# One transfer for the vectors and the first half of x, one for the first weights, decay preparation on GpSimd, and a bank read and three weight transfers placed sooner

## The chip, the core and the metric

The kernel runs on one core of one Trainium2 chip. A core has five engines with an instruction queue each: TensorE (PE in the profile; its weight loads are PEld), VectorE (DVE), ScalarE (ACT), GpSimd (POOL), and SyncE (SP), which here only asks for DMA transfers. The data lies in SBUF, 128 partitions wide; matmuls write to banks of PSUM. The metric is the device time of one execution in microseconds, as the median of several.

## What is computed

One layer of a hybrid decoder on 1024 tokens of width 1024, all in float32:

```python
z = rms_norm(h, norm_mix_g)
proj = z @ w_in                                  # 1024 -> 1536
y_pool = multiscale_pool_mixer(u_pool, ...)      # windows 2, 4, 8, 16
xb = causal_depthwise_conv(u_lru, conv_w, conv_b)
y_lru = rg_lru(xb, ...) * gelu(u_gate)           # log_a = 8 * r * log_sigmoid(lru_L)
h = h + concat([y_pool, y_lru]) @ w_out
z = rms_norm(h, norm_mlp_g)
h = h + square(relu(z @ w_up)) @ w_down          # 1024 -> 4096 -> 1024
z = rms_norm(h, norm_ple_g)
h = h + sigmoid(z @ w_ple_gate + b) * (p @ w_ple_proj)
return rms_norm(h, norm_final_g)
```

## The kernel before, in words

Activations stand transposed: the 1024 channels of x are eight tiles `H[k]` of 128 partitions, 1024 tokens wide. Every float32 product is made of three passes of a rounded format: an operand is split into a part `hi` (ScalarE, `split`, lines 180 and 183) and a rest `lo` (VectorE, lines 181 and 184), and `mm` (line 352) issues hi*hi, hi*lo and lo*hi as 128x512 matmuls. So nearly all matmuls have the same shape, and each needs a split by ScalarE and one by VectorE ahead of it. Weights come as raw tiles, two at a time, and their splits too lie in two buffers.

**The opening.** `vecs`, 80 columns of gains and biases (`COLS` names them), comes on ScalarE's queue (line 367). Nine matmuls on a tile `heat` keep TensorE busy meanwhile. Then a loop over k (line 487) loads `H[k]` and the weights `wl{k}` of the first projection (the recurrent channels): `H[0]` and `H[1]` in two halves of 512 tokens, the weights `wl0` in two cuts of 384 and 128 columns. All of these go through SyncE's queue, in the order of the program. For k = 0 the twelve matmuls of the first half come first, then the nine of the second half.

**Decay preparation.** `softplus` (line 454) works on tiles of 128x4: from `lru_L` it makes -8 log_sigmoid as `cpos` and its negative `cneg`, through an exponential on ScalarE and a series of nine steps, two operations each. It is issued at k = 2 on VectorE. `cneg` and `cpos` are first read by ScalarE in `lru_scan` (lines 612 and 613); `pool_bs`, the bias times the scale of the pooling mixer, in `pool_mix` (line 665).

**The mixer.** `project(i)` makes 48 matmuls into banks of PSUM. `normed` (line 552) reads the banks out on VectorE, times the inverse norm. `lru_gates(o)` makes twelve matmuls of 64 rows (line 592) into banks from the same pool, so these wait until an earlier result has been read out. The line in question is `normed(T[0], ps)` (line 689) after `lru_gates(2)`: it reads the result of `project(4)`, whose banks `lru_gates(3)` takes.

**The MLP.** Both products use a scheme with seven in place of eight block products (P1 to P7). The up product runs over 16 pairs of row tiles; `finish_up` (line 785) turns each pair's sums into operands of the down product and returns `store_up`, which writes them to DRAM tiles `act` by four transfers. The down product runs over the kinds P1, P2, P4, P6, P7, P5, P3, each with four steps q of 24 matmuls (`down`, line 960), twice. Its weights W[ij, q] are raw tiles loaded by `load_w`, its operands `wd` tiles X loaded back from `act` by `load_x` (line 295) and split by `prepare`. At P4 VectorE makes the sums that the later kinds take, first `w21 = w11 - w21` (line 214): that needs W[2, q]. W[2, 0] and W[2, 1] lie in T[2] and T[3], the tiles from which the last pair's first two stores read.

**What sets the order.** Within an engine the instructions run in the order that a scheduler has set from the program, with `tc.high_priority`, `tc.issue_after` and `pin` as means to move single ones. SyncE's queue is one such order: a transfer that has to wait for something holds up all transfers behind it.

Of the kernel before, what the change touches and what calls it, by code (L numbers as in the profile page):

```python
# [7 lines left out]
F32 = mybir.dt.float32  # L8
# [3 lines left out]
ALU = mybir.AluOpType  # L12

P = 128
S = 1024
D = 1024
DFF = 4096
HALF = 512
# [3 lines left out]
URGENT = 200  # L22
# [7 lines left out]
NT = D // P  # L30
# [9 lines left out]
NPOOL = 4  # L40
# [15 lines left out]
NVEC = _n  # L56
# [3 lines left out]
def block_kernel(  # L60
# [1 line left out]
    tc: tile.TileContext,  # L62
    xT: bass.AP,
    pT: bass.AP,
    vec: bass.AP,
    rows: bass.AP,
    w_lru: bass.AP,
    w_in: bass.AP,
# [9 lines left out]
    nc = tc.nc  # L78
# [5 lines left out]
    def fixed(name, dt):  # L84
        return pool.tile([P, S], dt, name=name)

    h_all = pool.tile([P, NT, S], F32, name="h")
    H = [h_all[:, i] for i in range(NT)]
    t_all = pool.tile([P, 6, S], F32, name="t")
    T = [t_all[:, i] for i in range(6)]  # L90

# [9 lines left out]
    def space(name, n, dt, side="left"):  # L101

        spaces[name] = ExitStack()
        sb = spaces[name].enter_context(tc.tile_pool(name=name, bufs=1, side=side))
        return [sb.tile([P, S], dt, name=f"{name}{i}") for i in range(n)]
# [5 lines left out]
        return list(zip(tiles[::2], tiles[1::2]))  # L111

    R = fixed("rstd", F32)
    dram = ctx.enter_context(tc.tile_pool(name="act", bufs=1, space=bass.MemoryType.DRAM))

    ACT = [
# [49 lines left out]
    def col(name, i):  # L166
        c = COLS[name] + i
        return vecs[:, c : c + 1]
# [3 lines left out]
    def pin(ins):  # L172
        return tc.keep_in_program_order(ins) if in_order else ins
# [3 lines left out]
    def split(src, hi, lo, g=None, eng=None):  # L177

        if g is None:
            first = pin(nc.scalar.activation(hi, src, AF.Copy))  # L180
            lowest[:] = [pin((eng or nc.vector).tensor_tensor(lo, src, f32(hi), ALU.subtract)).ins]  # L181
        else:
            first = pin(nc.scalar.activation(hi, src, AF.Identity, scale=g))
            lowest[:] = [pin(nc.vector.scalar_tensor_tensor(lo, src, g, f32(hi), ALU.mult, ALU.subtract)).ins]
        return first.ins

    def raw_tile(name):
        return wp.tile([P, S], F32, tag="raw", name=f"{name}_raw")
# [98 lines left out]
    def load_w(c, ij, q):  # L287
        if c < NCHUNK:
            nc.sync.dma_start(W[ij, q], w_down[c, ij, q])
# [73 lines left out]
        return t[:, k * P : (k + 1) * P]  # L363


    vecs = pool.tile([P, NVEC], F32, name="vecs")
    nc.scalar.dma_start(vecs, vec)
    heat = pool.tile([P, P], BF16, name="heat")
    tc.keep_in_program_order(nc.vector.memset(heat, 1.0))
    nc.vector.memset(T[4][:, :P], 1.0)  # L370
# [82 lines left out]
    def softplus():  # L453

        c0 = COLS["lru_l"]
        lv = vecs[:, c0 : c0 + NLRU]
        with tc.issue_after(lowest[0]):
            nc.vector.tensor_scalar_mul(neg, lv, -1.0)
        nc.vector.tensor_tensor(e, lv, neg, ALU.max)
        nc.scalar.activation(e, e, AF.Exp, scale=-1.0)  # L460
        nc.vector.tensor_scalar_add(s, e, 2.0)
        nc.vector.reciprocal(s, s)
        nc.vector.tensor_tensor(s, s, e, ALU.mult)
        nc.vector.tensor_tensor(s2, s, s, ALU.mult)
        nc.vector.memset(poly, 1.0 / 19)
        for n in range(8, -1, -1):
            nc.vector.tensor_tensor(poly, poly, s2, ALU.mult)
            nc.vector.tensor_scalar_add(poly, poly, 1.0 / (2 * n + 1))
        nc.vector.tensor_tensor(poly, poly, s, ALU.mult)
        nc.vector.tensor_scalar(neg, neg, 0.0, 8.0, ALU.max, ALU.mult)  # L470
        nc.vector.scalar_tensor_tensor(cpos, poly, 16.0, neg, ALU.mult, ALU.add)
        nc.vector.tensor_scalar_mul(cneg, cpos, -1.0)

        c_b, c_s = COLS["pool_b"], COLS["pool_s"]
        with tc.issue_after(lowest[0]):
            nc.vector.tensor_tensor(pool_bs, vecs[:, c_b : c_b + NPOOL], vecs[:, c_s : c_s + NPOOL], ALU.mult)

    norm = Norm("n0", T[0], T[1:3])
    ps_n = bank("n0_ps")
# [5 lines left out]
    for k in range(NT):  # L485
        halves = HALVES if k < 2 else (slice(0, S),)
        if k == 1:
            whi, wlo = weights()
        for hs in halves:
            begin = k == hs.start == 0  # L490
            nc.sync.dma_start(H[k][:, hs], xT[k * P : (k + 1) * P, hs])
            if begin:
                raw = raw_tile("wl0")[:, :HALF]
                whi, wlo = (t[:, :HALF] for t in weight_tiles("wl0"))
                cuts = slice(0, 3 * P), slice(3 * P, HALF)
                for cut in cuts:
                    nc.sync.dma_start(raw[:, cut], w_lru[:P, cut])
                pin(nc.vector.tensor_copy(whi[:, cuts[0]], raw[:, cuts[0]]))
            split(H[k][:, hs], A[k][0][:, hs], A[k][1][:, hs], col("g_mix", k))
            if k > 1:  # L500
                whi, wlo = weights()
            if begin:
                cut = cuts[0]
                pin(nc.vector.tensor_tensor(wlo[:, cut], raw[:, cut], f32(whi[:, cut]), ALU.subtract))
                split(*(t[:, cuts[1]] for t in (raw, whi, wlo)))
        for i in AFTER[k] if k < len(AFTER) else (k,):
            norm.add(H[i])
        if k == NT - 1:
            in_order.clear()
            ask()  # L510
        if k == 2:
            softplus()
        if k == 3:
            tables()
        if k == 5:
            pin(nc.scalar.activation(spread[:, 71:72], eps, AF.Sqrt))
        if k < 2:

            for hs in HALVES:
                for o in range(3):  # L520
                    mm(ps_l[o], kblk(whi, o), kblk(wlo, o), *A[k], k == 0, False, hs)
                if hs == FIRST:
                    mm([(FIRST, ps_four)], kblk(whi, 3), kblk(wlo, 3), *A[k], k == 0, False)
            continue
        for o in range(3):
            if k == NT - 1 and o == 2:
                norm.rstd(R, norm.sums((FIRST,), into=ps_n))
            mm(ps_l[o], kblk(whi, o), kblk(wlo, o), *A[k], False, k == NT - 1)
# [21 lines left out]
    def normed(dst, parts):  # L550
        for hs, ps in parts:
            nc.vector.tensor_tensor(by(dst[:, hs], ps), got(ps), by(R[:, hs], ps), ALU.mult)

# [132 lines left out]
    pool_windows(2, None)  # L686
    ps = project(4)
    lru_gates(2)
    normed(T[0], ps)
    ps = project(5)  # L690
    last = lru_gates(3)
    with tc.issue_after(last):
# [261 lines left out]
    def down(n):  # L954
        c, kind = KINDS[n]
        last = c == NCHUNK - 1

        def operand(t):
            return half(A[4 * (n % 2) + t // 2], t % 2)

        for q in range(NQ):
            w = weights() if n or q else asked.pop(0)
            if last and kind == "P5":
                if q == 0:
                    for k in range(2):
                        nc.sync.dma_start(T[4 + k], pT[k * P : (k + 1) * P, :])
                        nc.sync.dma_start(T[2 + k], w_proj[k * P : (k + 1) * P, :])
                elif q == 2:
                    open_ple()
            c11, c12, c21, c22 = (H[d][:, hs] for d in (2 * q, 2 * q + 1) for hs in HALVES)  # L970
            u = T[q // 2][:, HALVES[q % 2]]
            x = mlp_bank(f"ps_{kind}_d{c}_{q}")
            product(x, w, operand, range(CHUNK // 2), CHUNK // 2)
            if n == q == 0:
                leave("w0")
                S2[:] = *space("s2", 2, F32), *T[4:]
                finish_up(*done.pop())()
                for ij, i in ((1, 2), (1, 3), (3, 0), (2, 0), (3, 1), (2, 1)):
                    load_w(0, ij, i)
            if n == 1 and q in (1, 2):  # L980
                for ij in (3, 2):
                    load_w(0, ij, 1 + q)
            if kind == "P1":
                copy(u, x)
                add_got(c11, x)
            elif kind == "P2":
                add_got(c11, x)
            elif kind == "P6":
                add_got(u, x)
                add(c12, u)  # L990
            elif kind == "P7":
                add_got(u, x)
                add(H[2 * q + 1].rearrange("p (y s) -> p y s", y=2), twice(u))
            elif kind == "P4":
                add_got(c21, x)
            elif kind == "P5":
                add_both(h_all[:, 2 * q : 2 * q + 2, SECOND], x)
            else:
                add_got(c12, x)
            for tp in AHEAD[q] if n else AHEAD[q - 1]:  # L1000
                prepare(n + 1, tp)
            if last:
                for o in IN.get((kind, q), ()):
                    ple_in(o, FIRST, norm2)
                if (kind, q) == ("P3", 2):
                    norm2.casts((FIRST,))
# [392 lines left out]
```

## Time and profile before

| what | us |
|---|---|
| median of 3 runs | 922.6 (922.36 to 922.85) |
| the profiled execution, its own time | 922.75 |
| its span in the profile | 921.0 |
| TensorE busy in the span | 911.3 |
| VectorE busy | 762.5 |
| ScalarE busy | 444.5 |
| GpSimd busy | 8.0 |

The span runs from the first instruction to the last; 1.75 us of the profiled execution's time lie around it. A row of a timeline gives the start in us from the span's start, the time taken, the engine, the line, what it writes and reads, and in brackets how long the engine sat idle before it and what ended that. The letter q behind an engine is its queue: SPq rows are transfers being asked for, not their landing.

### The profile page before, as it was taken

Reading aid. Unit: us, or ns where it says so; the run is one execution under the profiler, and the core shown is the slowest. Engines: PE = TensorE matmul, PEld = TensorE weight load, DVE = VectorE, ACT = ScalarE, POOL = GpSimd, SP = SyncE. Lnnn points to the kernel's source line nnn. Section 1 sums busy time; section 2 is a strip of 40 time slices with the busy share of each in tenths; the row PEclk is TensorE's granted clock in tenths of the full one; section 3 lists DMA queues with packets and bytes.
Section 4 is the critical chain, followed back from the end, with each engine's and each line's share of the span. In section 5 each row is a group of like instructions: output and inputs, shape, how many; then the busy total and the mean of one; then the engine's idle time right before and its main releaser. Section 6 shows DMA issues by size and latency. Waiting matters only on the chain.

```text
span 921.0 us, 10988 instructions
## 1 busy us (share of the span) xinstructions
PE 911.3 (99%) x4229; PEld 792.4 (86%) x4229; DVE 762.5 (83%) x914; ACT 444.5 (48%) x516; POOL 8.0 (1%) x11
## 2 busy tenths in 40 slices
PE   9999999999999999999999999999999999999996
PEld 7888888888888888888888888888888888888886
DVE  7998984659998888888888989979777579789666
ACT  6567992447543343334333654444343346556223
POOL 0000000002000000000000000000000000000001
PEclk9999999999999999999999999999999999999999
DMA  7210143111245345435533988356533341031353
GB/s 272 93 54 32 38 161 114 69 46 51 88 166 189 126 154 195 154 126 175 198 131 145 315 329 328 129 186 203 192 123 119 114 161 46 1 121 63 105 174 121
DMA packets 50180, 129.07 MB, mean 140 GB/s; under 512 B 4560, under 2 KB 10192, under 8 KB 50128
## 3 DMA queue, kind: packets, MB, share of 16 engines
q1 hardware_dynamic: 49984, 128.34, 40.5%
q8 instruction: 33, 0.54, 0.2%
q14 instruction: 19, 0.16, 0.1%
q10 hardware_dynamic: 144, 0.04, 0.0%
HBM read 92.71 MB, written 35.65 MB: 139 GB/s over the span
## 4 chain that ended last, share of the span: by engine, by line
PE 85%; DVE 8%; DMA 3%; ACT 2%; issue 2%; SPq 0%; POOLq 0%; POOL 0%; ACTq 0%; DVEq 0%
PE ps_P_u L352 30%; PE ps_P_d L352 28%; PE ps_o L352 9%; PE ps_e L352 8%; PE ps_i L352 3%; PE ps_l L352 3%; PE ps_e L1163 2%; DMA wd<-act 2%; DVE h L565 2%; PE ps_j L352 1%; DMA wd<-in_w_down 1%; DVE y L181 1%; DVE wi_lo L181 1%; DMA h<-in_xT 1%; DVE t L647 1%
## 5 line engine op out<-in xcount | busy, mean ns | idle before, releaser
L352 PE MATMUL ps_P_d<-a,wd_P_hi 128*128 128x512 f32 x880 | 261.7, 379 | 0.0
L352 PEld LDWEIGHTS ps_P_d<-a,wd_P_hi 128*128 128x128 f32 x880 | 166.3, 189 | 23.6
L352 PE MATMUL ps_P_d<-a,wd_P_lo 128*128 128x512 f32 x440 | 166.9, 379 | 1.0 <-DVE wd_P_lo L181 1.0
L352 PE MATMUL ps_P_u<-a,wu_hi 128*128 128x512 f32 x512 | 152.3, 379 | 0.0
L352 PE MATMUL ps_P_u<-y,wu_hi 128*128 128x512 f32 x384 | 114.2, 379 | 0.0
L352 PEld LDWEIGHTS ps_P_u<-a,wu_hi 128*128 128x128 f32 x512 | 96.8, 189 | 13.8
L352 PE MATMUL ps_P_u<-a,wu_lo 128*128 128x512 f32 x256 | 97.0, 379 | 0.0
L352 PEld LDWEIGHTS ps_P_d<-a,wd_P_lo 128*128 128x128 f32 x440 | 83.2, 189 | 13.1 <-DVE wd_P_lo L181 1.4
L352 PEld LDWEIGHTS ps_P_u<-y,wu_hi 128*128 128x128 f32 x384 | 72.6, 189 | 10.3
L771 DVE TENSOR_TENSOR t<-t,ps_P_u 128x512 f32<-128x512 f32 (+1 forms) x80 | 62.5, 782 | 20.4 <-PE ps_P_u L352 20.4
L352 PE MATMUL ps_P_u<-y,wu_lo 128*128 128x512 f32 x192 | 72.8, 379 | 0.0
L180 ACT ACTIVATE a<-wd 128x1024 fp32r<-128x1024 f32 x56 | 59.0, 1055 | 24.2 <-DMA wd<-act 15.8
L181 DVE TENSOR_TENSOR a<-wd,a 128x1024 fp32r<-128x1024 f32 x56 | 67.2, 1220 | 1.0 <-ACT a L180 0.6
L352 PE MATMUL ps_i<-a,wi_hi 128*128 128x512 f32 x256 | 66.1, 381 | 0.0
L352 PE MATMUL ps_o<-y,wo_hi 128*128 128x512 f32 x256 | 65.7, 379 | 0.0
L180 ACT ACTIVATE wu_hi<-wu 128x1024 fp32r<-128x1024 f32 x24 | 25.4, 1058 | 69.8 <-PE ps_P_u L352 44.1
L180 ACT ACTIVATE wu_hi<-wu_raw 128x1024 fp32r<-128x1024 f32 (+1 forms) x26 | 25.3, 975 | 66.3 <-PE ps_P_u L352 41.3
L352 PEld LDWEIGHTS ps_i<-a,wi_hi 128*128 128x128 f32 x256 | 48.1, 189 | 8.0 <-issue 0.7
L352 PEld LDWEIGHTS ps_P_u<-a,wu_lo 128*128 128x128 f32 x256 | 48.4, 189 | 6.9
L352 PEld LDWEIGHTS ps_o<-y,wo_hi 128*128 128x128 f32 x256 | 48.4, 189 | 6.8
L180 ACT ACTIVATE wd_P_hi<-wd 128x1024 fp32r<-128x1024 f32 x24 | 25.3, 1053 | 48.2 <-PE ps_P_d L352 48.1
L771 DVE TENSOR_TENSOR h<-h,ps_P_d 128x512 f32<-128x512 f32 (+1 forms) x40 | 31.6, 790 | 19.1 <-PE ps_P_d L352 19.1
(255 smaller groups left out, 1493.6 us busy)
## 6 DMA issues: line engine op xcount, KB each, us to landing
wd<-act SPq DMA_DIRECT2D x56, 512.0 KB, 5.5
act<-t SPq DMA_DIRECT2D x32, 512.0 KB, 4.5
wu_raw<-in_w_up SPq DMA_DIRECT2D x16, 512.0 KB, 3.9
wu<-in_w_up SPq DMA_DIRECT2D x16, 512.0 KB, 4.0
act<-wu SPq DMA_DIRECT2D x16, 512.0 KB, 4.9
wd<-in_w_down SPq DMA_DIRECT2D x16, 512.0 KB, 6.3
h<-in_xT SPq DMA_DIRECT2D x14, 512.0 KB, 4.4
wg_raw<-in_w_gate SPq DMA_DIRECT2D x10, 512.0 KB, 3.1
```

The lines of the kernel that those rows point to most:

```text
L180: first = pin(nc.scalar.activation(hi, src, AF.Copy))
L181: lowest[:] = [pin((eng or nc.vector).tensor_tensor(lo, src, f32(hi), ALU.subtract)).ins]
L352: ins = nc.tensor.matmul(ps, w, turns(z[:, hs]), start=first and z is zhi and w is whi, stop=last and w is wlo, skip_group_check=more,)
L565: nc.vector.scalar_tensor_tensor(xb[:, j:], u[:, : S - j], col("conv_w", 4 * o + TAPS - 1 - j), xb[:, j:], ALU.mult, ALU.add,)
L647: nc.vector.tensor_tensor_scan(cur[:, w:], u[:, w:], u[:, : S - w], cur[:, w - 1 : w], ALU.add, ALU.subtract)
L771: (eng or nc.vector).tensor_tensor(to, to if y is None else y, x, ALU.add)
L1163: nc.tensor.matmul(pg, z, turns(w[:, k]), start=k == n == 0, stop=k == NT - 1 and n == 2)
```

## The change

The host lays the 80 vector columns and the first 512 tokens of the first 128 channels side by side into one input, `vec_x`. On the chip they land in one tile, in which `H` now follows the vectors, by one transfer that is SyncE's first; `wl0` comes whole by its second; the transfers of the vectors on ScalarE's queue, of `H[0]`'s first half and of the two cuts go. In `softplus` all but five small operations (four of VectorE, one of ScalarE) are issued on GpSimd; the sum of `cpos`, one operation before, is two. The read of the banks at line 689 gets a high priority. In `down`, three of the six loads W[1,2], W[1,3], W[3,0], W[2,0], W[3,1], W[2,1] are issued ahead of the last pair's `finish_up` and its four stores.

```diff
@@ -62,7 +62,7 @@
     tc: tile.TileContext,
     xT: bass.AP,
     pT: bass.AP,
-    vec: bass.AP,
+    vec_x: bass.AP,
     rows: bass.AP,
     w_lru: bass.AP,
     w_in: bass.AP,
@@ -84,8 +84,6 @@
     def fixed(name, dt):
         return pool.tile([P, S], dt, name=name)
 
-    h_all = pool.tile([P, NT, S], F32, name="h")
-    H = [h_all[:, i] for i in range(NT)]
     t_all = pool.tile([P, 6, S], F32, name="t")
     T = [t_all[:, i] for i in range(6)]
 
@@ -111,6 +109,10 @@
         return list(zip(tiles[::2], tiles[1::2]))
 
     R = fixed("rstd", F32)
+    start = pool.tile([P, NVEC + NT * S], F32, name="h")
+    vecs = start[:, :NVEC]
+    h_all = start[:, NVEC:].rearrange("p (i s) -> p i s", i=NT)
+    H = [h_all[:, i] for i in range(NT)]
     dram = ctx.enter_context(tc.tile_pool(name="act", bufs=1, space=bass.MemoryType.DRAM))
 
     ACT = [
@@ -363,8 +365,9 @@
         return t[:, k * P : (k + 1) * P]
 
 
-    vecs = pool.tile([P, NVEC], F32, name="vecs")
-    nc.scalar.dma_start(vecs, vec)
+    nc.sync.dma_start(start[:, : NVEC + HALF], vec_x)
+    raw_first = raw_tile("wl0")[:, :HALF]
+    nc.sync.dma_start(raw_first, w_lru[:P])
     heat = pool.tile([P, P], BF16, name="heat")
     tc.keep_in_program_order(nc.vector.memset(heat, 1.0))
     nc.vector.memset(T[4][:, :P], 1.0)
@@ -457,23 +460,24 @@
         with tc.issue_after(lowest[0]):
             nc.vector.tensor_scalar_mul(neg, lv, -1.0)
         nc.vector.tensor_tensor(e, lv, neg, ALU.max)
+        nc.vector.tensor_scalar(neg, neg, 0.0, 8.0, ALU.max, ALU.mult)
         nc.scalar.activation(e, e, AF.Exp, scale=-1.0)
-        nc.vector.tensor_scalar_add(s, e, 2.0)
+        nc.gpsimd.tensor_scalar_add(s, e, 2.0)
         nc.vector.reciprocal(s, s)
-        nc.vector.tensor_tensor(s, s, e, ALU.mult)
-        nc.vector.tensor_tensor(s2, s, s, ALU.mult)
-        nc.vector.memset(poly, 1.0 / 19)
+        nc.gpsimd.tensor_tensor(s, s, e, ALU.mult)
+        nc.gpsimd.tensor_tensor(s2, s, s, ALU.mult)
+        nc.gpsimd.memset(poly, 1.0 / 19)
         for n in range(8, -1, -1):
-            nc.vector.tensor_tensor(poly, poly, s2, ALU.mult)
-            nc.vector.tensor_scalar_add(poly, poly, 1.0 / (2 * n + 1))
-        nc.vector.tensor_tensor(poly, poly, s, ALU.mult)
-        nc.vector.tensor_scalar(neg, neg, 0.0, 8.0, ALU.max, ALU.mult)
-        nc.vector.scalar_tensor_tensor(cpos, poly, 16.0, neg, ALU.mult, ALU.add)
-        nc.vector.tensor_scalar_mul(cneg, cpos, -1.0)
+            nc.gpsimd.tensor_tensor(poly, poly, s2, ALU.mult)
+            nc.gpsimd.tensor_scalar_add(poly, poly, 1.0 / (2 * n + 1))
+        nc.gpsimd.tensor_tensor(poly, poly, s, ALU.mult)
+        nc.gpsimd.tensor_scalar_mul(cpos, poly, 16.0)
+        nc.gpsimd.tensor_tensor(cpos, cpos, neg, ALU.add)
+        nc.gpsimd.tensor_scalar_mul(cneg, cpos, -1.0)
 
         c_b, c_s = COLS["pool_b"], COLS["pool_s"]
         with tc.issue_after(lowest[0]):
-            nc.vector.tensor_tensor(pool_bs, vecs[:, c_b : c_b + NPOOL], vecs[:, c_s : c_s + NPOOL], ALU.mult)
+            nc.gpsimd.tensor_tensor(pool_bs, vecs[:, c_b : c_b + NPOOL], vecs[:, c_s : c_s + NPOOL], ALU.mult)
 
     norm = Norm("n0", T[0], T[1:3])
     ps_n = bank("n0_ps")
@@ -488,14 +492,13 @@
             whi, wlo = weights()
         for hs in halves:
             begin = k == hs.start == 0
-            nc.sync.dma_start(H[k][:, hs], xT[k * P : (k + 1) * P, hs])
             if begin:
-                raw = raw_tile("wl0")[:, :HALF]
+                raw = raw_first
                 whi, wlo = (t[:, :HALF] for t in weight_tiles("wl0"))
                 cuts = slice(0, 3 * P), slice(3 * P, HALF)
-                for cut in cuts:
-                    nc.sync.dma_start(raw[:, cut], w_lru[:P, cut])
                 pin(nc.vector.tensor_copy(whi[:, cuts[0]], raw[:, cuts[0]]))
+            else:
+                nc.sync.dma_start(H[k][:, hs], xT[k * P : (k + 1) * P, hs])
             split(H[k][:, hs], A[k][0][:, hs], A[k][1][:, hs], col("g_mix", k))
             if k > 1:
                 whi, wlo = weights()
@@ -686,7 +689,8 @@
     pool_windows(2, None)
     ps = project(4)
     lru_gates(2)
-    normed(T[0], ps)
+    with tc.high_priority(URGENT):
+        normed(T[0], ps)
     ps = project(5)
     last = lru_gates(3)
     with tc.issue_after(last):
@@ -974,8 +978,10 @@
             if n == q == 0:
                 leave("w0")
                 S2[:] = *space("s2", 2, F32), *T[4:]
+                for ij, i in ((1, 2), (1, 3), (3, 0)):
+                    load_w(0, ij, i)
                 finish_up(*done.pop())()
-                for ij, i in ((1, 2), (1, 3), (3, 0), (2, 0), (3, 1), (2, 1)):
+                for ij, i in ((2, 0), (3, 1), (2, 1)):
                     load_w(0, ij, i)
             if n == 1 and q in (1, 2):
                 for ij in (3, 2):
@@ -1370,7 +1376,7 @@
     ins = {
         "xT": c(np.asarray(x)[0].T),
         "pT": c(np.asarray(p)[0, 0].T),
-        "vec": c(vec),
+        "vec_x": np.concatenate([c(vec), np.asarray(x)[0].T[:P, :HALF]], axis=1),
         "rows": c(np.concatenate(rows)).reshape(1, -1),
         "w_lru": c(first),
         "w_in": tiles(rest),
```

How this moves the instructions, at three places. The first is the head of SyncE's queue; h is the tile of the vectors and x, wl0_raw and wl1_raw are the raw first weights. Before:

```order
L491 DMA h_67<-in_xT 128x512
L497 DMA wl0_raw_163<-in_w_lru 128x384
L497 DMA wl0_raw_163<-in_w_lru 128x128
L491 DMA h_67<-in_xT 128x512
L198 DMA wl1_raw_198<-in_w_lru 128x512
L491 DMA h_67<-in_xT 128x512 x2
L491 DMA h_67<-in_xT 128x1024
```

And with the change:

```order
L368 DMA h_71<-in_vec_x 128x592
L370 DMA wl0_raw_138<-in_w_lru 128x512
L501 DMA h_71<-in_xT 128x512
L200 DMA wl1_raw_195<-in_w_lru 128x512
L501 DMA h_71<-in_xT 128x512 x2
L501 DMA h_71<-in_xT 128x1024
```

The second half of `H[0]` is third in the queue where it was fourth, and all behind it move up by one. The second place is VectorE's queue around the bank read; ps_i4 is the result of `project(4)`, wi6 the weights of `project(6)`, y the split operands of later products. Before:

```order
L181 TENSOR_TENSOR y3_116<-t_68,y2_115 128x1024
L181 TENSOR_TENSOR y5_118<-t_68,y4_117 128x1024
L181 TENSOR_TENSOR wi6_lo_902<-wi6_raw_900,wi6_hi_901 128x1024
L552 TENSOR_TENSOR t_68<-ps_i4_0_826,rstd_71 128x512
L552 TENSOR_TENSOR t_68<-ps_i4_512_827,rstd_71 128x512
```

And with the change:

```order
L183 TENSOR_TENSOR y3_116<-t_67,y2_115 128x1024
L555 TENSOR_TENSOR t_67<-ps_i4_0_824,rstd_70 128x512
L555 TENSOR_TENSOR t_67<-ps_i4_512_825,rstd_70 128x512
L183 TENSOR_TENSOR wi6_lo_900<-wi6_raw_898,wi6_hi_899 128x1024
L183 TENSOR_TENSOR y5_118<-t_67,y4_117 128x1024
```

The two reads pass two full-width splits. The third place is SyncE's queue where the up product ends and the down product begins; act1 are the last pair's stores, wd12, wd13 and wd4 are W[1,2], W[1,3] and W[3,0], t is W[2,0] and W[2,1], wd5 is W[3,1], and wd0 is the first operand tile of P4. Before:

```order
L295 DMA wd3_3847<-act0_1_3_81 128x2x512
L806 DMA act1_0_3_93<-t_68 128x1024
L806 DMA act1_1_3_97<-t_68 128x1024
L806 DMA act1_2_3_101<-wu0_1740 128x1024
L807 DMA act1_3_3_105<-wu1_1741 128x512
L289 DMA wd12_3857<-in_w_down 128x1024
L289 DMA wd13_3858<-in_w_down 128x1024
L289 DMA wd4_3848<-in_w_down 128x1024
L289 DMA t_68<-in_w_down 128x1024
L289 DMA wd5_3849<-in_w_down 128x1024
L289 DMA t_68<-in_w_down 128x1024
L295 DMA wd0_3844<-act0_2_0_82 128x2x512
```

And with the change:

```order
L297 DMA wd3_3845<-act0_1_3_81 128x2x512
L291 DMA wd12_3855<-in_w_down 128x1024
L291 DMA wd13_3856<-in_w_down 128x1024
L291 DMA wd4_3846<-in_w_down 128x1024
L810 DMA act1_0_3_93<-t_67 128x1024
L810 DMA act1_1_3_97<-t_67 128x1024
L810 DMA act1_2_3_101<-wu0_1738 128x1024
L811 DMA act1_3_3_105<-wu1_1739 128x512
L291 DMA t_67<-in_w_down 128x1024
L291 DMA wd5_3847<-in_w_down 128x1024
L291 DMA t_67<-in_w_down 128x1024
L297 DMA wd0_3842<-act0_2_0_82 128x2x512
```

The three loads pass the four stores; W[2,0] stands where it stood, behind seven transfers. GpSimd's queue gains 27 operations of 128x4 ahead of its first full tile, 25 of them in one chain. Apart from these places, some single operations of the last kind (P3) of the down product and of the gate's operands change places on VectorE and ScalarE, and one early matmul on TensorE.

## The prediction

> **What bounds the kernel now.** I read the page's head first, then the chain of waits, then the timelines of the places where the chain leaves TensorE.
>
> ```profile
> span 921.0 us, 10988 instructions
> PE 911.3 (99%) x4229; PEld 792.4 (86%) x4229; DVE 762.5 (83%) x914; ACT 444.5 (48%) x516; POOL 8.0 (1%) x11
> 2.15 4.71 DMA h<-in_xT
> 6.88 0.73 ACT a L183
> 7.63 0.76 DVE a L184
> 8.44 28.54 PE ps_l L352 x131
> ...
> 250.82 256.42 PE ps_P_u L352 x1188
> ```
>
> TensorE is the bound: its longest piece holds 1188 matmuls in 256.42 us, 0.216 us each, so it runs without a gap there. A change can only pay where matmuls stand further apart than that, and must cost where it makes a gap. The windows say where gaps are:
>
> ```profile
> 0.00:9.00 9.00, 7.50 (x25) 3.85 (x26) 3.64 (x10) 4.41 (x7) 0.20 (x4) 1.00 0.67 218
> 14.00:37.00 23.00, 23.00 (x108) 20.16 (x107) 22.54 (x49) 16.69 (x20) 0.00 (x0) 1.00 0.45 161
> 507.00:541.00 34.00, 34.00 (x160) 29.76 (x159) 31.09 (x32) 20.72 (x24) 0.00 (x0) 1.00 0.96 336
> 541.00:556.00 15.00, 14.04 (x66) 11.97 (x65) 11.32 (x12) 6.96 (x7) 0.00 (x0) 1.00 0.70 257
> ```
>
> After the stretch and its length the columns are busy time of PE, PEld, DVE, ACT and POOL, the granted clock (1.00, so no throttle), the DMA share and GB/s. TensorE lacks time in the first 9 us and 0.96 us after 541, and none from 14 to 37. A third place, near 107 us, shows in its timeline. The change touches all three.
>
> **First place: the opening.** The chain rows above read: the second half of `H[0]` is asked for at 2.15 and there at 6.86; ScalarE's split, VectorE's split, and from 8.44 TensorE runs at full rate.
>
> ```profile
> 1.19 0.92 SPq L497 DMA_DIRECT2D wl_raw<-in_w_lru  x2
> 7.41 0.38 PE L352 MATMUL ps_l<-a,wl_lo 128*128 128x512 f32 x1
> 3.76 0.72 ACT L183 ACTIVATE a<-h,vecs 128x512 fp32r<-128x512 f32 x1 [1.10 <-DMA h<-in_xT]
> 4.09 0.36 DVE L498 CAST wl_hi<-wl_raw 128x384 fp32r<-128x384 f32 x1 [2.69 <-DMA wl_raw<-in_w_lru]
> ```
>
> One transfer fewer ahead of that half is one issue slot: the two cuts of the weights fill 1.19 to 2.15, so 0.48 us each. The bytes ahead stay the same, so how much the landing moves is unknown. Gain at most: the first half's twelve matmuls end with the one at 7.41, at 7.63; the next two could follow at 7.63 and 7.85 where the second now starts at 8.44, so 0.59. Loss at most: the first half starts on the first two landings, seen at 3.76 and 4.09; the second transfer's 192 KB came 0.33 us behind the first, so the 40 KB and 64 KB that the two now carry more are 0.07 and 0.11 us, 0.2 together. I take the slot, 0.48, nearer to the upper end because the chain names this landing alone. What follows has room: the next k's splits sit behind landings that move by the same slot.
>
> **Second place: the bank read.**
>
> ```profile
> 95.09 0.59 PE L352 MATMUL ps_i<-a,wi_lo 128*128 128x512 f32 x2
> 97.11 0.48 PE L352 MATMUL ps_i<-a,wi_hi 128*128 128x512 f32 x1
> 107.14 0.59 PE L352 MATMUL ps_i<-a,wi_lo 128*128 128x512 f32 x2
> 107.97 1.85 PE L592 MATMUL ps_g<-y,hl 64*128 64x512 f32 x12 [0.24 <-DVE t L552]
> 109.76 0.48 PE L352 MATMUL ps_i<-a,wi_hi 128*128 128x512 f32 x1
> 103.76 2.33 DVE L181 TENSOR_TENSOR y<-t,y 128x1024 fp32r<-128x1024 f32 x2
> 106.01 1.22 DVE L181 TENSOR_TENSOR wi_lo<-wi_raw,wi_hi 128x1024 fp32r<-128x1024 f32 x1
> 107.15 1.28 DVE L552 TENSOR_TENSOR t<-ps_i,rstd 128x512 f32<-128x512 f32 x2
> ```
>
> The same piece of TensorE's program, gates between two projections, takes 97.11 - 95.09 = 2.02 us undisturbed and 109.76 - 107.14 = 2.62 here: 0.60 lost to the reads, which end at 108.43. Ahead of two splits they end 2.3 us earlier, near 106.1, before TensorE comes: 0.60 gained. The passed splits cost nothing: wi_lo, for the projection that starts at 109.76, moves from 107.23 to about 107.4, and the y tile to 108.5, with no reader before TensorE's next mixing. Without that cover wi_lo would cost its lateness. Bounds: 0.60, and 0 if another read holds the banks. I take 0.60.
>
> **Third place: the start of the down product.**
>
> The last row is from the table of DMA issues: its last number is the median from issue to landing. The others are from the timelines.
>
> ```profile
> 553.04 0.59 PE L352 MATMUL ps_P_d<-a,wd_P_hi 128*128 128x512 f32 x2
> 553.47 0.38 PE L352 MATMUL ps_P_d<-a,wd_P_lo 128*128 128x512 f32 x1
> 553.68 0.59 PE L352 MATMUL ps_P_d<-a,wd_P_hi 128*128 128x512 f32 x2
> 555.24 0.48 PE L352 MATMUL ps_P_d<-a,wd_P_lo 128*128 128x512 f32 x1 [0.96 <-DVE wd_P_lo L181]
> 544.69 1.23 DVE L214 TENSOR_TENSOR t<-w_raw,t 128x1024 f32<-128x1024 f32 x1 [3.65 <-DMA t<-in_w_down]
> 517.51 4.30 SPq L295 DMA_DIRECT2D wd<-act  x4
> 528.37 0.80 SPq L806 DMA_DIRECT2D act<-t  x2
> 534.29 0.38 SPq L289 DMA_DIRECT2D t<-in_w_down  x1
> t<-in_w_down SPq DMA_DIRECT2D x4, 512.0 KB, 8.5
> ```
>
> After a pair of hi matmuls the lo follows 0.43 us later; here 1.56: 1.13 lost, 1.23 with the slow matmul behind. VectorE brings wd_P_lo late because it sat 3.65 us until W[2,0] had landed at 544.69, and from there worked without a pause. So the price hangs on that one landing. W[2,0] overwrites what the first store reads, so it is asked for only when that store is through, at 534.29.
>
> With the change W[1,2], W[1,3] and W[3,0] go out between 521.81, when SyncE falls idle, and 528.37, when the stores' data is ready. They stand in the same queue, so W[2,0] has the same seven transfers ahead. What is gained is what the DMA engines idled: a share of 0.96 leaves 0.04, and over the 21 us from 523 to 544 that is 0.85 us. Gain at most 1.23 (the gap gone). Loss at most: the first store now lies behind three transfers of 512 KB, 1.56 us each at 336 GB/s; so W[2,0] is asked for at 534.29 + 4.7 = 539.0, and after the row's 8.5 us lands at 547.5, 2.8 late. I take the 0.85: a transfer's landing in a full queue is set by the bytes ahead, not by when it was asked for.
>
> [...]
>
> **The rest.** The decay preparation; the first row is the window 14 to 37 for the sp tiles alone, the others are from the timelines:
>
> ```profile
> 14.00:37.00 23.00, 3.94 (x25) 1.00 0.45 161
> 83.85 1.15 ACT L612 ACTIVATE h<-h,sp 128x1024 f32<-128x1024 f32 x1
> 211.71 3.45 DVE L181 TENSOR_TENSOR a<-t,a 128x1024 fp32r<-128x1024 f32 x2 [0.53 <-ACT a L180]
> 212.28 1.79 POOL L217 TENSOR_TENSOR rstd<-wu_raw 128x512 f32<-128x512 f32 x1 [211.84 <-DMA wu_raw<-in_w_up]
> 904.67 0.94 POOL L1199 TENSOR_TENSOR edge<-edge,power 128x1 f32<-128x1 f32 x1 [3.66 <-DVE edge L1143]
> 911.15 0.55 POOL L1199 TENSOR_TENSOR edge<-edge,power 128x1 f32<-128x1 f32 x1 [5.54 <-DVE edge L1143]
> 905.18 0.68 DVE L1153 TENSOR_TENSOR late<-late,t 128x512 f32<-128x512 f32 x1
> 31.14 1.28 DVE L184 SCALAR_TENSOR_TENSOR a<-h,vecs,a 128x1024 fp32r<-128x1024 f32 x1
> ```
>
> The first row is the window of the sp tiles alone: VectorE is rid of nearly all of 3.94 us. TensorE has no gap there, so that gains nothing. GpSimd's 25 chained operations, at 0.55 to 0.94 each from 14 us on, end by 38, and 83.85 is their first reader: hidden. VectorE's reciprocal waits for one of them, some 0.5 us, and behind it waits the split for k = 3; the split for k = 7 (last row) has about 2 us of room, worked out below, and I take the same here. The reorderings around P3 lie far ahead of their matmuls: nothing.
>
> **Sum** against the profiled execution's 922.75: 0.48 + 0.60 + 0.85 = 1.93, so 920.82; the median lies 0.15 below, so 920.7.
>
> **Rivals.**
> - *Everything closes.* The opening gives 0.59 and the third gap closes whole, 1.23: with 0.60 it is 2.42, 920.2. For it: both gaps hang on one landing each.
> - *The transfers only change places.* The third term is 0: 1.08, 921.5. For it: the share of 0.96 says the engines had hardly an idle moment, and the slowest of sixteen decides a landing. Against it: 6.56 us of SyncE idling.
> - *W[2,0] late.* The 2.8 us of the lower bound, less 1.08: +1.7, 924.3. Against it: those 8.5 us are mostly time in the queue.
> - *GpSimd holds up VectorE in the opening.* Slower. At 211.71 two splits took 3.45 where two take 2.33 (row 103.76): 1.1 lost to a GpSimd operation that itself took 1.79. From 14 to 37 VectorE is busy 22.54 of 23 us. Its 49 operations there less the 25 small ones leave 24, about 19 of them with two full SBUF inputs; if each lets one small GpSimd operation in for 0.55 us, that is 10.5 less the 3.8 freed, 6.7 late. The split for k = 7 ends at 32.42; its matmuls are the last twelve of the 131 up to 36.98, so from 34.4 on: 2 us of room. TensorE then stalls 4.7, less 1.93: 925.4. It decides from 0.3 us each. Against it: in row 904.67 it was the small operation that took 0.94 for 0.55, while VectorE's neighbour (905.18) kept its 0.68.
>
> [...]
>
> **How the numbers follow.** The forecast (920.7, own range 920.2 to 921.3) 0.45; everything closes 0.15; only places 0.22; W[2,0] late 0.06; GpSimd 0.07; something unseen 0.05. A difference below 0.2%, 1.85 us, is about what a measurement of this kernel can tell from no change. 920.75 is that border, so the forecast splits: 0.30 of its 0.45 faster, with the whole of the second case 0.45; no change 0.43 from the rest, the second rival and some of the late ones; slower 0.12. The range, 919.9 to 922.9, holds the first three cases and a small loss at the third place.
>
> **What would show it.** TensorE's full rate starting near 8.0 instead of 8.44; the gates piece near 107 us taking 2.0; VectorE's wait for W[2,0] below 3 us and the lo gap near 553 below 0.5. In the opening VectorE's splits should keep 1.28 and TensorE stay gapless to 37. The prediction is wrong if splits there grow, if the first matmuls start later than 4.6, or if W[2,0] lands later after the P1 matmuls than before.

## The result, and the profile after

| | before | after |
|---|---|---|
| median of 19 runs each, us | 922.48 (921.24 to 923.54) | 920.76 (920.06 to 923.2) |
| ratio of the times | | 0.9986 (95%: 0.998 to 0.9993) |
| the profiled execution, us | 922.75 | 920.58 |
| TensorE busy | 911.3 | 910.5 |
| VectorE busy | 762.5 | 759.7 |
| GpSimd busy | 8.0 | 25.2 |

The kernel is 0.14% faster, some 1.3 us by the ratio, with an interval of 0.6 to 1.8 us; a gain below 0.2% counts as no change. (The two medians lie 1.72 us apart, which is inside that interval.) The two profiled executions lie 2.17 us apart. That difference between one pair of executions and the repeated timing is what most of the experiments are about.

The chain of waits of the changed kernel begins so (start, length, what):

```profile
2.59 5.64 DMA h<-in_xT
8.25 0.73 ACT a L185
9.00 0.76 DVE a L186
9.81 26.60 PE ps_l L354 x122
```

The transfer named is now the first half of `H[1]`, asked for at 2.59, no longer the second half of `H[0]`: a new wait stands behind the one that went. The piece that reaches the end of the first projection ends at 9.81 + 26.60 = 36.41, where it ended at 36.98 before: 0.57 sooner. The windows, with the columns of the prediction:

```profile
0.00:9.00 9.00, 7.96 (x29) 4.97 (x30) 3.67 (x9) 4.52 (x8) 0.49 (x6) 1.00 0.77 262
14.00:37.00 23.00, 23.00 (x108) 20.10 (x107) 20.31 (x26) 16.44 (x21) 17.19 (x24) 1.00 0.47 163
507.00:541.00 34.00, 34.00 (x159) 29.79 (x158) 30.10 (x31) 19.41 (x23) 0.00 (x0) 1.00 0.95 341
541.00:556.00 15.00, 15.00 (x71) 12.91 (x70) 13.53 (x14) 8.12 (x8) 0.00 (x0) 1.00 0.88 304
```

TensorE is busy 7.96 of the first 9 us (7.50 before), still without a gap from 14 to 37, and from 541 on it lacks nothing (0.96 before). GpSimd's 17.19 us in the second row are the decay preparation. TensorE's timeline at its first matmuls, at the new wait, at the bank read and at the start of the down product:

```profile
4.68 1.36 PE L354 MATMUL ps_l<-a,wl_hi 128*128 128x512 f32 x5
...
9.12 0.38 PE L354 MATMUL ps_l<-a,wl_lo 128*128 128x512 f32 x1
9.33 0.96 PE L354 MATMUL ps_l<-a,wl_hi 128*128 128x512 f32 x2
10.13 0.38 PE L354 MATMUL ps_l<-a,wl_lo 128*128 128x512 f32 x1
...
106.57 0.59 PE L354 MATMUL ps_i<-a,wi_lo 128*128 128x512 f32 x2
107.09 1.56 PE L595 MATMUL ps_g<-y,hl 64*128 64x512 f32 x12
108.58 1.13 PE L354 MATMUL ps_i<-a,wi_hi 128*128 128x512 f32 x4
...
552.50 0.59 PE L354 MATMUL ps_P_d<-a,wd_P_hi 128*128 128x512 f32 x2
552.98 0.48 PE L354 MATMUL ps_P_d<-a,wd_P_lo 128*128 128x512 f32 x1
```

The pair at 9.33 takes 0.96 where such pairs take 0.59: the first matmul of `H[1]`'s lo waits for the split that the chain shows. From the lo pair at 106.57 to the next projection it is now 108.58 - 106.57 = 2.01 us (2.62 before): 0.6 gained. At the down product the lo follows its pair after 0.48 (1.56 before). VectorE's timeline shows both causes:

```profile
104.29 1.28 DVE L555 TENSOR_TENSOR t<-ps_i,rstd 128x512 f32<-128x512 f32 x2
105.49 1.22 DVE L183 TENSOR_TENSOR wi_lo<-wi_raw,wi_hi 128x1024 fp32r<-128x1024 f32 x1
...
542.44 1.23 DVE L216 TENSOR_TENSOR t<-w_raw,t 128x1024 f32<-128x1024 f32 x1 [2.58 <-DMA t<-in_w_down]
```

The reads are done at 105.57, ahead of the weights' rest. The wait for W[2,0] fell from 3.65 to 2.58. In this pair of executions the three places thus gave 0.57, 0.60 and 1.1.

### The profile page after: what moved, and what is told of

It is laid out like the page before. It is cut to its first block, busy times and chain, and to the rows that moved or that the text cites. A ratio compares the mean times of both kernels' runs of the same rounds, so it can differ in the third digit from the quotient of the medians.

```text
span 918.8 us, 10986 instructions
## 1 busy us (share of the span) xinstructions
PE 910.5 (99%) x4229; PEld 792.5 (86%) x4229; DVE 759.7 (83%) x888; ACT 444.7 (48%) x516; POOL 25.2 (3%) x38
## 4 chain that ended last, share of the span: by engine, by line
PE 97%; DMA 1%; issue 1%; DVE 0%; ACT 0%; SPq 0%; POOLq 0%; POOL 0%; ACTq 0%
PE ps_P_d L354 32%; PE ps_P_u L354 32%; PE ps_i L354 9%; PE ps_o L354 9%; PE ps_e L354 8%; PE ps_l L354 3%; PE ps_e L1169 2%; PE ps_j L354 1%; PE ps_g L595 1%; DMA h<-in_xT 1%; PE ps_p L354 1%; PE ps_l_second L354 1%; PE ps_j L1178 0%; PE n_ps L421 0%; PE n_ps L422 0%
## 5 line engine op out<-in xcount | busy, mean ns | idle before, releaser
L182 ACT ACTIVATE a<-wd 128x1024 fp32r<-128x1024 f32 x56 | 58.9, 1053 | 25.2 <-DMA wd<-act 16.3
L182 ACT ACTIVATE wu_hi<-wu_raw 128x1024 fp32r<-128x1024 f32 (+1 forms) x26 | 25.2, 974 | 66.3 <-PE ps_P_u L354 41.3
```

## The experiments

### One part of the change at a time

Four kernels, each the kernel before with one part. The opening's transfers (the lines that go with them are left out here):

```diff
-    nc.scalar.dma_start(vecs, vec)
+    nc.sync.dma_start(start[:, : NVEC + HALF], vec_x)
+    nc.sync.dma_start(raw_first, w_lru[:P])
...
```

> The kernel before with the opening's transfers of the change alone (vectors and first half of H[0] in one, wl0 in one). Theory (one issue slot and the first landings): TensorE's full rate starts 0.5 to 0.6 us sooner, as in the full change (0.57), held back by the first half of H[1] as there; 922.75 becomes 922.2, a ratio of 0.9994. Rival (the gain needs the decay preparation off VectorE, whose small operations stand among the splits for k = 2 and 3): gain under 0.3, or a gap that opens between 14 and 37 us. At the down product's start the gap is to be as before, 1.1 lost behind W[2,0], if the order of the transfers makes it; if it hangs on when a packet of another queue (16 KB in 1.03 us at 542.1 before, at 538.7 with the change) falls into that landing, it may come out between 0 and 1.2 here though no order there is changed.

The bank read:

```diff
-    normed(T[0], ps)
+    with tc.high_priority(URGENT):
+        normed(T[0], ps)
```

> The kernel before with the priority on the one bank read alone. Theory: the gates piece near 107 us takes 2.0 instead of 2.6, so 0.60 sooner from there to the end, 922.15, ratio 0.9993. Rival (the late wi_lo split gives it back): a gap of 0.2 to 0.6 at the first matmuls of the next projection. The gap at the down product's start as in the expectation of the opening's kernel: 1.1 by the order of the transfers, anything from 0 to 1.2 by the packet of the other queue.

The three weights:

```diff
+                for ij, i in ((1, 2), (1, 3), (3, 0)):
+                    load_w(0, ij, i)
                 finish_up(*done.pop())()
-                for ij, i in ((1, 2), (1, 3), (3, 0), (2, 0), (3, 1), (2, 1)):
+                for ij, i in ((2, 0), (3, 1), (2, 1)):
```

> The kernel before with W[1,2], W[1,3], W[3,0] ahead of the last pair's stores alone. Theory (order): W[2,0] is asked for 3 to 4 us later and lands 1 to 1.3 sooner against TensorE's work, the lo gap near 553 falls from 1.34 us between starts to below 0.5, gain 1.07, 921.7, ratio 0.9988. Rival (chance): the landing depends on when the 16 KB packet of the other queue falls on it; then the gap stays above 0.6 here in spite of the order, and the gain is 0 to 0.7.

The decay preparation:

```diff
-        nc.vector.tensor_scalar_add(s, e, 2.0)
+        nc.gpsimd.tensor_scalar_add(s, e, 2.0)
...
-        nc.vector.scalar_tensor_tensor(cpos, poly, 16.0, neg, ALU.mult, ALU.add)
+        nc.gpsimd.tensor_scalar_mul(cpos, poly, 16.0)
+        nc.gpsimd.tensor_tensor(cpos, cpos, neg, ALU.add)
```

> The kernel before with the decay preparation on GpSimd alone. Theory: no gap of TensorE changes up to 500 us, 922.75 within 0.2, ratio 1.0000; the small GpSimd operations wait beside VectorE's (1.0 to 1.3 us each in place of 0.2), VectorE's splits keep 1.28 and 1.22. Rival 1 (GpSimd holds VectorE up): splits of 1.6 and more between 14 and 33 us and a gap before 37. Rival 2 (VectorE's relief helps): up to 0.3 sooner by 37 us. The gap at the down product's start: 1.1 lost by the order of the transfers, 0 to 1.2 by the packet.

| part alone | ratio (95%) | us, by the ratio |
|---|---|---|
| opening | 0.9993 (0.9984 to 1.0001) | -0.65 |
| bank read | 0.9991 (0.9982 to 1.0) | -0.83 |
| weights | 1.0001 (0.9993 to 1.001) | +0.09 |
| decay | 1.0002 (0.9993 to 1.0011) | +0.18 |

No interval excludes no change, but the four add up to -1.2, near the whole change's -1.3. The order of the weights, worth 1.07 in the first pair of profiles, shows nothing: its interval ends at a gain of 0.65. The traces say why: with the order of before, the loss near 553 is gone in the opening's and in the decay's kernel too, though nothing was changed there, and all but gone in the bank read's. Distances between starts near 553 were below 0.33 us in all three. The opening's kernel ends the first projection's piece at 36.61, 0.37 sooner than the first profile of before and 0.74 sooner than the mean of six old openings. The decay's kernel had the latest of these, 38.15, because its second half of `H[0]` landed at 8.03; that is 6 us before the chain of its decay preparation begins, at 14.17, so it is hardly due to that (of the part, only two operations of 0.1 and 0.2 us on GpSimd run earlier).

In the weights' kernel W[2,0] was asked for later, as the order wants it, and its landing stayed where it was. SyncE's timeline and VectorE's, of that kernel and then of the opening's, which has the old order:

```profile
539.23 0.33 SPq L289 DMA_DIRECT2D t<-in_w_down  x1
543.51 1.23 DVE L214 TENSOR_TENSOR t<-w_raw,t 128x1024 f32<-128x1024 f32 x1 [1.83 <-DMA t<-in_w_down]
```

```profile
534.97 0.33 SPq L291 DMA_DIRECT2D t<-in_w_down  x1
543.09 1.22 DVE L216 TENSOR_TENSOR t<-w_raw,t 128x1024 f32<-128x1024 f32 x1 [2.44 <-DMA t<-in_w_down]
```

W[2,0] is asked for 4.3 us later and the work behind its landing starts 25.45 us after the down product's first matmul, against 26.05: the prediction's argument that the bytes ahead set a landing in a full queue fits this. Over all profiles it is 25.5 to 26.2 with the new order, and with the old one 25.5 to 26.6, apart from two executions at 27.2 and 27.3, which the section after the next takes up.

The bank read, by contrast, gave its whole amount. Its kernel's timeline of TensorE, the same place as above:

```profile
107.03 0.59 PE L352 MATMUL ps_i<-a,wi_lo 128*128 128x512 f32 x2
107.56 1.56 PE L592 MATMUL ps_g<-y,hl 64*128 64x512 f32 x12
109.05 1.13 PE L352 MATMUL ps_i<-a,wi_hi 128*128 128x512 f32 x4
```

109.05 - 107.03 = 2.02. Over all profiles of this study the time from the first gates matmul to the first matmul of the down product is 458.82 to 458.87 us with the old read (eight profiles) and 458.25 to 458.27 with the new one (six).

### The change without the weights, and without the decay preparation

Two kernels, each the full change with one part undone (the diffs are the third and fourth above, reversed).

> The full change with the three weights put back behind the last pair's stores. In the four kernels run so far TensorE's loss at the start of the down product was 0.10 and below, with the old order of these transfers (three kernels) as with the new; only the profile of before lost 1.23. Theory (chance: the loss comes and goes from one execution to the next): here too it comes out below 0.5, the time stays that of the full change within 0.3 us, near 920.9, ratio 0.9986. Rival (order, the prediction's third term): 1.07 slower than the full change, 921.8, ratio 0.9995 or above, with a gap of 1 us and more between starts near 553.

> The full change with the decay preparation back on VectorE. Theory: no part of the gain hangs on it; the time is that of the full change, 920.8, ratio 0.9986, TensorE gapless from 14 to 37 us as before. Rival (VectorE's relief helps the opening): 0.3 or more slower, seen as a gap of TensorE before 37 us. It also gives another look at the new opening (boundary of the first gates piece near 57.8; 58.1 to 59.4 in the four looks at the old) and at the new order of the weights (loss below 0.2).

Both have the time of the full change: 0.9986 (0.9977 to 0.9995) without the weights, 0.9984 (0.9975 to 0.9993) without the decay preparation. TensorE waits for nothing near 553 in either, and has no gap from 14 to 37 us in the second. So neither part is seen to be needed for the gain, within intervals some 0.8 us wide to either side.

### The kernels themselves, profiled again

Is the loss of 1.23 a property of the kernel before, or of one execution of it? The kernel before was profiled twice more, the changed one once.

> The kernel before, unchanged, for a second profile of it. Theory (the loss of 1.23 at the start of the down product came and went with the execution): below 0.5 here, with W[2,0] landing less than 26.6 us after the down product's first matmul (27.25 in the first profile, 25.4 to 26.6 in the others). Rival (it belongs to this kernel): 1.0 to 1.3 again. The opening's boundary of the first gates piece may come anywhere from 57.9 to 59.5.

> The changed kernel, unchanged, for a second profile of it. Theory: bank read as before (2.02, no loss); loss at the start of the down product below 0.2; boundary of the first gates piece between 57.6 and 58.5 (57.68, 57.88, 58.41 and 58.09 in the four looks at this opening). Rival (the first profile's 2.2 us under the kernel before is what the change is worth): span 918.8 within 0.3 again.

> The kernel before, unchanged, a third profile. The loss at the start of the down product was 1.23 and 1.19 in its two profiles and 0 to 0.23 in six profiles of other kernels with the same order of these transfers. Theory (it comes and goes with the execution, in this kernel too): below 0.5 here or in the fastest of its timed runs at least, since a run of 921.1 lies 1.65 under the first profile's 922.75 and the opening can give only 1.04 of that (its first matmul to the first gates piece took 53.66, at best 52.62). Rival (it belongs to this kernel's program): 1.0 to 1.3 a third time, W[2,0] 2.8 behind W[3,0].

First the second profile of the kernel before: the view of TensorE's waits (waiting for what: us in total, times, longest), then VectorE's wait for W[2,0].

```profile
PE ps_P_d L352 <- DVE wd_P_lo L181: 0.9, 1, 0.9
```

```profile
545.58 1.23 DVE L214 TENSOR_TENSOR t<-w_raw,t 128x1024 f32<-128x1024 f32 x1 [3.61 <-DMA t<-in_w_down]
```

The third profile of the same kernel has no wait of TensorE there, and this wait of VectorE:

```profile
542.85 1.23 DVE L214 TENSOR_TENSOR t<-w_raw,t 128x1024 f32<-128x1024 f32 x1 [2.20 <-DMA t<-in_w_down]
```

So after the second profile the rival (it belongs to this program) stood; the third took it down. One kernel, three executions: 3.65, 3.61 and 2.20 us of waiting, and 1.2, 1.2 and 0 lost. From the start of the down product's first matmul to the end of the program's last it is 396.5, 396.5 and 395.3 us in them, and in the six other kernels with the old order 395.3 to 395.9. With the new order five profiles show 395.3 to 395.4. That the late landing came in two of nine executions with the old order and in none of five with the new one is too little to say that the order prevents it. Both late ones are of the kernel before itself, two of its three, and none of the six other kernels' with the old order; so it is not excluded that this program has the late landing more often than its neighbours.

The opening scatters as well. Chains of waits, of the second profile of the kernel before:

```profile
2.14 5.65 DMA h<-in_xT
9.38 28.54 PE ps_l L352 x131
```

of the third:

```profile
2.14 4.32 DMA h<-in_xT
8.05 28.54 PE ps_l L352 x131
```

and of the changed kernel's second:

```profile
1.04 3.83 PE ps_l L488 x9
4.87 31.23 PE ps_l L354 x144
```

The same transfer, asked for at 2.14, took 5.65 in one execution and 4.32 in the other, and the piece behind it ends at 37.92 and 36.59. In the changed kernel's second profile no DMA stands in the chain at all: from the first warming matmul to the end of the first projection, at 36.10, TensorE sets its own pace. That execution took 920.15 us with a span of 918.4, and the boundary that the expectation names, the start of the last matmul ahead of the first gates piece, lay at 57.39. The theory's 57.6 to 58.5 for it and the rival's span of 918.8 within 0.3 were both missed on the fast side. The chains of three other profiles with this opening (the opening's kernel and the full change without the weights and without the decay preparation) hold no DMA up to the end of that piece either, at 36.61, 37.13 and 36.82: what is left of the opening is then TensorE's own start (last section).

### Which part of the opening?

The kernel before with the vectors merged into the first transfer, and wl0 still in two cuts:

```diff
-    nc.sync.dma_start(raw_first, w_lru[:P])
+    for cut in (slice(0, 3 * P), slice(3 * P, HALF)):
+        nc.sync.dma_start(raw_first[:, cut], w_lru[:P, cut])
```

(against the opening's kernel above.)

> The kernel before with the vectors merged into the first transfer, but wl0 still in two cuts, so the second half of H[0] stays fourth in SyncE's queue. Theory of the slot (the second half gains because it is third in the queue): nothing gained, the second half of H[0] lands as in the four looks at the old order (6.3 to 8.0), boundary of the first gates piece 58.1 to 59.4, ratio 1.000. Rival (the gain is the separate transfer of the vectors on the other queue, 128 packets of 320 bytes, going away): landing near 6.0 and the boundary near 57.8, ratio 0.9993.

And the kernel before with wl0 whole, the vectors apart:

```diff
-                for cut in cuts:
-                    nc.sync.dma_start(raw[:, cut], w_lru[:P, cut])
+                nc.sync.dma_start(raw, w_lru[:P])
```

> The kernel before with wl0 in one transfer instead of two cuts, and nothing else: the vectors stay apart on ScalarE's queue, the second half of H[0] is third in SyncE's queue. Theory of the slot: that half is asked for 0.48 us sooner and lands as in the looks with the full opening (5.2 to 6.1, four looks), the loss behind it before the matmuls of the second half is gone (0 where the old order lost 0 to 1.55 in four looks), ratio 0.9993. Rival (the vectors' own transfer disturbs the first landings; merging it alone gave a landing of 6.18 and a ratio of 0.9992 with the half still fourth): landing 6.3 to 8.0 as in the old order, ratio 1.000.

The times are 0.9992 (0.9983 to 1.0001) and 0.9994 (0.9985 to 1.0003): neither can be told from no change, nor from the other. The chains differ. Wl0 whole:

```profile
1.66 5.41 DMA h<-in_xT
8.65 28.54 PE ps_l L352 x131
```

Vectors merged:

```profile
1.05 4.02 PE ps_l L488 x9
5.08 31.82 PE ps_l L354 x144
```

With wl0 whole the second half of `H[0]` is asked for at 1.66, a slot of 0.48 sooner, and still lands at 7.07, among the old openings; TensorE waits for it. With the vectors merged it is asked for at 2.12, as before, and ScalarE starts its split at 6.21, 0.15 earlier than in the earliest of the six old openings; nothing waits, though the piece ends at 36.90 because the first matmuls were slow in this execution (last section). By these two profiles the vectors' own transfer would be what counts, not the slot. The next experiment speaks against so plain an answer: with the vectors merged and the slot gained, that half landed at 7.18 there. One profile each decides nothing, given the scatter, and which of the two moves the landing stays open.

### The first half of H[1] ahead of its weights

On the full change, for the new wait:

```diff
         if k == 1:
+            nc.sync.dma_start(H[1][:, FIRST], xT[P : 2 * P, FIRST])
+            split(H[1][:, FIRST], A[1][0][:, FIRST], A[1][1][:, FIRST], col("g_mix", 1))
             whi, wlo = weights()
-        for hs in halves:
+        for hs in halves[1:] if k == 1 else halves:
```

> The full change with the first half of H[1] asked for, and split, ahead of the weights wl1. In the profile of the full change TensorE's matmuls for k = 1 stand 0.26 us late (474 ns where 216 is the rule) because the split of that half waits for a landing at 8.22 while the weights landed at 7.57. Theory: up to 0.26 gained, 920.5, ratio 0.9984. Rival (the weights' split becomes the last one instead): 0 within 0.1, with a gap of the same size that the weights' rest ends.

0.9987 (0.9979 to 0.9996), the time of the full change. In its one profile the second half of `H[0]` landed at 7.18 and TensorE waited for that, so the wait that this edit was to remove could not show. Up to that half's transfer its queue is that of the full change, and the next one is of the same size, so it is a sixth execution of the new opening's landing, and it falls among the old ones (6.34 to 8.03). Whether the edit is worth anything stays open; no version here beats the full change by more than the noise.

## Why the prediction was right, and where it was not

The predicted 920.7 stands against 920.76, and of the signs that it lists for the profile all but two came out. The first matmuls start at 4.68, where 4.6 was the limit named. And the full rate did not start near 8.0: TensorE runs at it from about 5 us on and loses 0.26 at the pair at 9.33, which comes to the same gain. But the sum reached the number with two sizes wrong in opposite directions, and that it met the median so closely is in good part luck: a gain of 1.93 was forecast, and by the ratio it is 1.3.

| place | predicted | first pair of profiles | all profiles | part alone, timed |
|---|---|---|---|---|
| opening | 0.48 | 0.57 | 0.7 | 0.6 |
| bank read | 0.60 | 0.60 | 0.60 | 0.8 |
| weights | 0.85 | 1.07 | 0.4 | -0.1 |
| decay | 0 | 0 | 0 | -0.2 |

*All profiles* is the difference of means of the end of the first projection's piece (six old openings 37.35, from 36.59 to 38.15; five new ones 36.61, from 36.10 to 37.13), of the two ranges of the bank read above, and of the stretch from the down product on (nine with the old order 395.7, five with the new 395.3). The timed parts have intervals of some 0.8 us to either side.

**Opening.** The mechanism, the landing of the second half of `H[0]`, was right, and the 0.48 is near the first pair's 0.57. The cause given, one issue slot with the bytes unchanged, does not account for how far the landing moved: ScalarE starts that split at 7.18 on average over six old openings and at 5.56 over five new ones, 1.6 sooner for a slot of 0.48 (1.35 with the 7.20 of the last experiment as a sixth), and the slot alone left it at 7.09 in one profile. The loss that the lower bound allowed for came to half its size: the weights that the first matmuls need land at 4.30 on average, 4.19 before. *What follows has room* failed in the first pair, by the 0.26 that the pair at 9.33 loses: the first half of `H[1]` landed at 8.22, only 0.22 sooner than before, behind matmuls that had become 0.57 earlier. The bound of 0.59 above held for one execution only: the profile shown had its landing at 6.85, nearer to the early end than to the late end, 8.03.

**Bank read.** Right in every step: the reads end ahead of TensorE, the passed splits cost nothing, and the amount repeats to 0.05 us.

**Weights.** The step that failed is the price: *a loss of 1.23 hangs on that one landing*. It does, but only in some executions: where VectorE's wait is 3.6, TensorE loses 1.2; where it is 2.65 or less, at most 0.3 there. The profile that the sum was made from had the loss, and most executions do not have it. The 0.85 was taken from the DMA engines' idle share of 21 us; VectorE's wait did fall by 1.07 in the first pair, but with the old order it is 1.59 to 2.65 in seven of nine executions. The rival *the transfers only change places*, given 0.22, is what the timing shows (1.0001, and 0.85 lies outside the interval), and its 921.5 is 0.7 above the median. The runs before the change could have warned: a second execution at 922.36 lies 0.49 below the slowest, in a kernel whose gaps were priced to 0.1.

**Decay preparation.** Hidden, as said. The rival that GpSimd holds VectorE up fell: a small GpSimd operation next to a full VectorE one waited itself, 1.24 us in place of 0.20. GpSimd's timeline of the changed kernel, then VectorE's:

```profile
14.20 0.20 POOL L467 TENSOR_TENSOR sp<-sp 128x4 f32<-128x4 f32 x1 [0.30 <-DVE sp L466]
14.48 0.20 POOL L468 TENSOR_TENSOR sp<-sp 128x4 f32<-128x4 f32 x1
14.76 1.24 POOL L471 TENSOR_TENSOR sp<-sp 128x4 f32<-128x4 f32 x1
16.08 0.40 POOL L472 TENSOR_SCALAR sp<-sp 128x4 f32<-128x4 f32 x1
```

```profile
14.65 1.28 DVE L186 SCALAR_TENSOR_TENSOR a<-h,a 128x1024 fp32r<-128x1024 f32 x1 [0.53 <-ACT a L185]
```

Two operations of 0.20 start while VectorE is idle; the third, the same operation, starts 0.11 behind VectorE's split and takes 1.24, until that is through; the split keeps the 1.28 that it took in the profile before. That each of some 19 of VectorE's full operations would let a small one in was the author's estimate; VectorE's splits of x from 14 to 31 us take 1.20 to 1.29, where before they took 1.28 to 1.29. The chain ended at 33.34, with its first reader near 83.

**The sum.** 1.93 was to come off an execution of 922.75 that had lost 1.23 at a place where nine profiles with the old order lose 0.3 on average (the rest of the table's 0.4 is lost near 533, in two of the other kernels). The timed gain is 1.3.

## What to carry to other kernels

A gap behind a DMA landing, seen in one profile, is one draw (1.2, 1.2 and 0 us lost here in three executions of one kernel): profile the same kernel two or three times before pricing it, and compare the runs' scatter with the gap. A gap that an engine's own order makes, as the bank read's, repeated here to 0.05 us and can be priced from one profile. Of a change made of parts, time each alone: here the part with the largest predicted gain is one whose timing showed none.

## What the runs showed of the hardware that was not expected

**TensorE's first microseconds.** Two executions with the same opening, the change without the weights and the changed kernel's second profile; TensorE's timelines:

```profile
4.82 2.31 PE L354 MATMUL ps_l<-a,wl_hi 128*128 128x512 f32 x5
6.97 0.60 PE L354 MATMUL ps_l<-a,wl_lo 128*128 128x512 f32 x2
```

```profile
4.78 1.32 PE L354 MATMUL ps_l<-a,wl_hi 128*128 128x512 f32 x5
5.93 0.59 PE L354 MATMUL ps_l<-a,wl_lo 128*128 128x512 f32 x2
```

The same five matmuls take 6.97 - 4.82 = 2.15 us in one and 1.15 in the other, so 0.43 each in the first and 0.23 in the second, where 0.216 is the fast rate; the windows of the first show a granted clock of 1.00 all the same, in each us from 3 to 11. TensorE became fast at a different time in these two executions, and here that makes a difference of 1 us, more than the whole opening's gain. In the first of the two the fast rate came 5.9 us behind the first warming matmul, at 1.04, in the second within 4.9. What sets that time no run here shows.

**Landings in a full queue.** W[2,0] landed 2.83, 2.82 and 1.31 us behind W[3,0], next in the same queue, in three executions of one kernel. In the first of them fifteen of its sixteen landing signals came from 540.53 to 542.97 and the last at 544.67; VectorE's work behind it starts at 544.69, so the slowest of the sixteen decided that landing. A packet of 16 KB of another queue, which holds some DMA engine for 1.0 us, starts 1.0 to 2.6 us ahead of that landing in all three (542.1, 543.2 and 541.9), each time 0.3 to 0.4 us behind the landing of W[3,0], so its presence alone decides nothing; on which engine it falls the trace does not tell. What makes the landing late was not settled.
